# A split-operand product for the first halves of two modulation vectors, and an earlier load of the first projection's weights

## The chip, the cores and the metric

The kernel runs on one core of one Trainium2 chip. The metric is the device time of one execution in microseconds (us). The engines are named as in the profile: PE is TensorE (matrix products and transposes), PEld its weight loads, DVE is VectorE, ACT is ScalarE, POOL is GpSimd, and SP is SyncE, which in this kernel issues the DMAs. L312 is line 312 of the kernel before; the lines behind the change are 9 higher in the kernel after it.

## The reference

One inference step of a hybrid backbone, one layer deep: 128 context tokens and 2048 latent tokens of width 1024, taken here as 17 tiles of 128 tokens (tile 0 is the context). Cut to what matters:

```
def modulation(cond, w_mod, b_mod):                  # cond: 1024 values
    m = silu(cond) @ w_mod + b_mod                   # w_mod: 1024 x 6144
    return split(m, 6)                               # six vectors of 1024

def block(x, s0, mod, ...):
    sh1, sc1, ga1, sh2, sc2, ga2 = mod
    h = rmsnorm(x, norm_mix) * (1 + sc1) + sh1
    o, s_new = mixer(h, s0, ...)                     # one input projection, DeltaNet + gMLP, one output projection
    x = x + ga1 * o
    h = rmsnorm(x, norm_ffn) * (1 + sc2) + sh2
    return x + ga2 * (relu(h @ w_ff1)**2 @ w_ff2), s_new
```

Context and latent tokens have a conditioning vector each, so that each modulation vector comes in two rows. All is in 32-bit floats. Nothing of the mixer can start before h, and so not before `sh1` and `sc1`, the first two of the six vectors.

## The kernel before

**Products.** Large products are made of split operands: a float32 matrix is cast by ACT to the type fp32r (the high part `wH`, L191), DVE subtracts that from the original (the low part `wL`, L192), and PE multiplies high by high, high by low and low by high (`mm3`, L217 to L219), one pass each. `split_w` (L185) makes the two parts of one 128x512 tile. A product of plain float32 operands is a single call, which the trace shows as two passes of PE.

**Modulation vectors.** `scond` holds silu of the two conditioning vectors as eight columns of 128x2. The vectors are made in chunks of 512 columns of `w_mod`, each over eight tiles of 128x512 (256 KB; k0 to k7). The first four chunks are needed first and have their own path. `mod_load` (L306) issues the loads of a chunk: `m0` is the first half of `sh1`, `m1` the first half of `sc1`, `m2` and `m3` the second halves. `mod_columns` (L310) makes eight float32 products with `scond` as the stationary operand into two rows of PSUM (L314), copies them to SBUF on ACT (`mrow`, L316), turns them into columns by four transposes (L319), and adds the bias on DVE (L322; for `sc1` also the weight of the norm, L326). The results are `b1` and `a1`, which scale and shift the normalised tokens.

The chunks 4 to 9 of `w_mod` follow in single steps between the later work. `split_mod_steps` (L329) makes chunk 4, called jc = 4 here: each tile is split, and PE multiplies both parts (L338, L339) with `abW`, a 128x128 stationary operand for each k, most of which is zero. Its columns 32 to 34 hold the high part of `scond` and its columns 64 to 66 the low part (L301 to L304), so that the rows 32 to 34 and 64 to 66 of the result, added, make the two rows wanted. The columns 0 to 32 of `abW` take the small weights `abr` of the mixer, later.

**Tokens.** `xh` (10 rows at the edges of the blocks, L359) and then the tiles of the first block of three (0, 1, 2; loaded at L371) are normalised by `norm_rows` (L291): square and sum on ACT (L297), scale and epsilon on DVE (L175), the power -0.5 on POOL (L176), and the scaling on DVE (L299). The four share three buffers. `first_half` (L384) scales the edge rows by `a1` and `b1`; `column(k)` in `prep_block` (L448) transposes 128 columns of the three token tiles on PE (L461), applies `a1` and `b1` on ACT (L463), and splits the result on DVE (L466, L467). The first projection (`feature_tile`, products L217 to L219 into `pj`) multiplies these by the split tiles of `w_in`, called `W1`, loaded by `load_w1` (L376). The first four of these tiles are `wr` at L713.

**What sets the order.** The kernel names no queue order by hand. The tile framework takes the instructions in program order and orders those of each engine by a time model of its own, within the data's dependences. Buffers of a pool are passed on when their last reader is done: 49 of 128x512 in `wp` (the tiles of m0 to m3 and W1, and the parts of split tiles), four in `sp` ("stage": raw tiles and split parts of jc = 4, and raw tiles of weights that are split on arrival). All loads here go through SP, in one order. The program around the change is the start of the sequence (L707 on):

```
        blk, xs_, cols = prep_block(0)
        ...
        m2 = mod_load(1, 0)
        m3 = mod_load(1, D)
        wr = load_w1(1, range(4))
        mod_columns(m1, 0, a1, vec[:, 8:16], True)
        W1[1] += [split_w(r) for r in wr]
        first_half(0)
```

Ahead of it stand the loads of m0 and m1, `mod_columns` for m0 (L353), and the loads and norms of `xh` and of the three token tiles. Behind it come the other loads of W1, the first four columns of the block with the first products of three feature tiles (L721 to L725), `mod_columns` for m2 and m3 (L726, L727), and the rest of the mixer, block by block.

Of the kernel before, what the change touches and what calls it, by code (L numbers as in the profile page):

```python
# [13 lines left out]
ALU = mybir.AluOpType  # L14
# [5 lines left out]
KT = D // P  # L20
# [41 lines left out]
def hybrid_step(  # L62
# [7 lines left out]
    V, A, G, T = nc.vector, nc.scalar, nc.gpsimd, nc.tensor  # L70
# [12 lines left out]
    def f32(ap):  # L83
        return ap.bitcast(F32)
# [77 lines left out]
    scond = cp.tile([P, KT, 2], F32, name="scond")  # L162
# [6 lines left out]
    def pm1():  # L169
        return pmp.tile([P, 512], F32, tag="pm", name="pm", bufs=2)  # L170
# [9 lines left out]
    def raw_w(src, pool=None, tag="w"):  # L180
        t = (pool or wp).tile([P, 512], F32, tag=tag, name="raw")
        load(out=t, in_=src)
        return t

    def split_w(raw, scale=None, pool=None, tag="w"):  # L185

        h = (pool or wp).tile([P, 512], F32R, tag=tag, name="wH")
        lo = (pool or wp).tile([P, 512], F32R, tag=tag, name="wL")
        if scale is not None:
            V.tensor_scalar_mul(raw, raw, scale)  # L190
        A.copy(h, raw)  # L191
        V.tensor_tensor(out=lo, in0=raw, in1=f32(h), op=ALU.subtract)  # L192
        return h, lo
# [66 lines left out]
    with ExitStack() as ph:  # L260
# [40 lines left out]
        abW = p1.tile([P, KT, P], F32R, tag="abW", name="abW", bufs=1)  # L301
# [4 lines left out]
        def mod_load(half, c0):  # L306
            return [raw_w(w_mod[0, k * P : (k + 1) * P, c0 + half * 512 : c0 + half * 512 + 512])
                    for k in range(KT)]

        def mod_columns(raws, half, dst, bias, scaled):  # L310

            pm = pm1()  # L312
            for k in range(KT):
                T.matmul(pm[0:2, :], scond[:, k, :], raws[k], start=k == 0, stop=k == KT - 1)  # L314
            row = p1.tile([2, 512], F32, tag="mrow", name="mrow", bufs=1)
            A.copy(row, pm[0:2, :])  # L316
            pc = pm1()
            for i in range(4):
                T.transpose(pc[:, 2 * i : 2 * i + 2], row[:, i * P : (i + 1) * P], ident[0:2, 0:2])  # L319
            ks = slice(half * 4, half * 4 + 4)  # L320
            d = dst[:, :, ks]
            V.tensor_tensor(out=d, in0=pc[:, 0:8].rearrange("p (k c) -> p c k", c=2),  # L322
                            in1=bias[:, ks].unsqueeze(1).to_broadcast([P, 2, 4]), op=ALU.add)
            if scaled:
                for cd in range(2):
                    V.scalar_tensor_tensor(out=dst[:, cd, ks], in0=dst[:, cd, ks], scalar=1.0,  # L326
                                           in1=vec[:, 16 + half * 4 : 20 + half * 4], op0=ALU.add, op1=ALU.mult)
# [23 lines left out]
        convw = vec[:, 32:68].rearrange("p (w a) -> p w a", w=3)  # L351
        m1 = mod_load(0, D)
        mod_columns(m0, 0, b1, vec[:, 0:8], False)  # L353


# [20 lines left out]
        def load_w1(gi, ks):  # L376
            return [w1_raw(gi, k) for k in ks]

        def w1_raw(gi, k):
            return raw_w(w_in[0, k * P : (k + 1) * P, gi * 512 : (gi + 1) * 512])  # L380
# [327 lines left out]
        blk, xs_, cols = prep_block(0)  # L708
        for st in xs_:
            st()  # L710
        m2 = mod_load(1, 0)
        m3 = mod_load(1, D)
        wr = load_w1(1, range(4))  # L713
        mod_columns(m1, 0, a1, vec[:, 8:16], True)
        W1[1] += [split_w(r) for r in wr]
        first_half(0)
# [3 lines left out]
        wr = load_w1(0, range(KT))  # L720
        us = [feature_tile(blk, 0, 1, h) for h in range(3)]  # L721
        for k in range(4):
            cols[k]()
            for u in us:
                u["main"][k]()  # L725
        mod_columns(m2, 1, b1, vec[:, 0:8], False)  # L726
        mod_columns(m3, 1, a1, vec[:, 8:16], True)  # L727
        W1[1] += [split_w(r) for r in wk]
# [1015 lines left out]
    raws, sops = {}, {}  # L1744
# [46 lines left out]
    half = [p for p, e in enumerate(seq) if e[1] == NP][0]  # L1791
# [41 lines left out]
    for m, (n, i, u, q) in enumerate(todo):  # L1833
# [12 lines left out]
        h, lo = sops.pop(m)  # L1846
# [72 lines left out]
```

## Time and profile before

| | us |
|---|---|
| three runs | 2704.84, 2711.76, 2714.13 (median 2711.76) |
| profiled execution: its time | 2707.53 |
| profiled execution: its span | 2705.8 |
| products of the MLP (`f`, six groups L217 to L219), busy on PE | 2193.9 |
| products of the input projection (`pj` with `kH`, `kL`, three groups) | 571.4 |
| stretch 0 to 40.4 us of the span: PE busy | 33.41 |

The span is the time from the first to the last recorded instruction of one execution; its mean granted PE clock was 0.99 of full speed. Busy times of an engine's groups may add up to more than the engine's own, because successive products overlap in the records. The profile was read in these views: the page (busy time by engine, the chain of work that ended last), a table of stretches of the span (busy time of each engine, the clock granted to PE, share of the DMA engines and GB/s), and timelines of one engine at a time. In a timeline, a row gives the start and the duration in us (from the first start to the last end of the instructions grouped), the engine, the line, the operation, the result and the operands by their names in the program, shapes, and the count; in brackets stands the idle time of the engine just before, and what ended it. "SPq" is the issue of DMAs on SP.

### The profile page before, as it was taken

Reading aid. Unit: us, or ns where it says so; the run is one execution under the profiler, and the core shown is the slowest. Engines: PE = TensorE matmul, PEld = TensorE weight load, DVE = VectorE, ACT = ScalarE, POOL = GpSimd, SP = SyncE. Lnnn points to the kernel's source line nnn. Section 1 sums busy time; section 2 is a strip of 40 time slices with the busy share of each in tenths; the row PEclk is TensorE's granted clock in tenths of the full one; section 3 lists DMA queues with packets and bytes.
Section 4 is the critical chain, followed back from the end, with each engine's and each line's share of the span. In section 5 each row is a group of like instructions: output and inputs, shape, how many; then the busy total and the mean of one; then the engine's idle time right before and its main releaser. Section 6 shows DMA issues by size and latency. Waiting matters only on the chain.

```text
span 2705.8 us, 45189 instructions
## 1 busy us (share of the span) xinstructions
PE 2632.3 (97%) x15698; PEld 2196.5 (81%) x15698; DVE 1868.0 (69%) x3909; ACT 1246.1 (46%) x3092; POOL 228.2 (8%) x448
## 2 busy tenths in 40 slices
PE   8999998999999999999999999999999999999998
PEld 5999997788887787778888778888888787788887
DVE  5867656877777978985677857565565556775874
ACT  4655555555555667763355533332342432232441
POOL 3111213111111111110000000000000000000000
PEclk9999999999999999999999999999999999999999
DMA  8867539555555657875887786433459979776772
GB/s 296 279 199 223 185 115 294 179 159 155 163 162 172 212 180 245 268 263 175 286 234 232 213 299 206 123 102 109 117 174 371 326 262 308 267 239 216 233 258 91
DMA packets 569387, 580.91 MB, mean 215 GB/s; under 512 B 35692, under 2 KB 401692, under 8 KB 565574
## 3 DMA queue, kind: packets, MB, share of 16 engines
q1 hardware_dynamic: 569158, 578.03, 66.5%
q8 instruction: 123, 2.02, 0.3%
q14 instruction: 106, 0.87, 0.1%
HBM read 398.14 MB, written 179.74 MB: 214 GB/s over the span
## 4 chain that ended last, share of the span: by engine, by line
PE 82%; DMA 7%; DVE 6%; issue 2%; ACT 2%; SPq 1%; POOL 0%; DVEq 0%; POOLq 0%; ACTq 0%
PE f L219 16%; PE f L217 16%; PE f L218 16%; PE pj L217 6%; PE pj L219 6%; PE pj L218 6%; PE pd L952 3%; PE pm L217 1%; DMA qT<-qT_d 1%; PE pm L218 1%; PE pm L219 1%; PE pt L568 1%; PE pd L1129 1%; PE pd L1130 1%; PE pt L528 1%
## 5 line engine op out<-in xcount | busy, mean ns | idle before, releaser
L219 PE MATMUL f<-hop,zL 128*128 128x512 f32 x960 | 377.9, 394 | 1.7 <-DVE zL L1431 1.7
L217 PE MATMUL f<-hop,zH 128*128 128x512 f32 x960 | 377.6, 394 | 1.2 <-ACT zH L1437 1.2
L218 PE MATMUL f<-hop,zH 128*128 128x512 f32 x960 | 378.0, 394 | 0.0
L217 PE MATMUL f<-hop,wH 128*128 128x512 f32 x896 | 356.2, 398 | 5.8 <-ACT wH L1437 5.8
L219 PE MATMUL f<-hop,wL 128*128 128x512 f32 x896 | 352.2, 393 | 0.0
L218 PE MATMUL f<-hop,wH 128*128 128x512 f32 x896 | 352.0, 393 | 0.0
L1437 ACT CAST zH<-zraw 128x512 fp32r<-128x512 f32 x240 | 147.1, 620 | 299.2 <-DVE zraw L1431 91.9
L219 PEld LDWEIGHTS f<-hop,zL 128*128 128x128 f32 x960 | 180.9, 188 | 45.0 <-DVE zL L1431 3.5
L217 PEld LDWEIGHTS f<-hop,zH 128*128 128x128 f32 x960 | 180.7, 188 | 44.7 <-ACT zH L1437 2.9
L218 PEld LDWEIGHTS f<-hop,zH 128*128 128x128 f32 x960 | 180.6, 188 | 40.9
L1431 DVE TENSOR_TENSOR zL<-zraw,zH 128x512 fp32r<-128x512 f32 x240 | 162.6, 687 | 68.2 <-ACT zH L1437 50.8
L217 PEld LDWEIGHTS f<-hop,wH 128*128 128x128 f32 x896 | 169.4, 189 | 40.9 <-ACT wH L1437 6.2
L219 PEld LDWEIGHTS f<-hop,wL 128*128 128x128 f32 x896 | 169.0, 189 | 38.0 <-DVE wL L1431 0.3
L218 PEld LDWEIGHTS f<-hop,wH 128*128 128x128 f32 x896 | 169.4, 189 | 35.2
L217 PE MATMUL pj<-kH,wH 128*128 128x386 f32 (+2 forms) x568 | 191.0, 339 | 0.3 <-DVE kH L466 0.3
L219 PE MATMUL pj<-kH,wL 128*128 128x386 f32 (+2 forms) x568 | 190.6, 336 | 0.0
L218 PE MATMUL pj<-kL,wH 128*128 128x386 f32 (+2 forms) x568 | 189.8, 334 | 0.0
L176 POOL TENSOR_TENSOR r<-rsq,nhalf 128x1 f32<-128x1 f32 (+1 forms) x38 | 23.6, 621 | 1516.4 <-DVE rsq L175 1516.4
L1431 DVE TENSOR_TENSOR wL<-raw,wH 128x512 fp32r<-128x512 f32 x112 | 76.1, 687 | 76.0 <-ACT wH L1437 75.0
L516 DVE SCALAR_TENSOR_TENSOR cv<-pj,vec,cv 128x384 f32<-128x384 f32 (+2 forms) x164 | 87.1, 539 | 59.9 <-ACT cv L513 58.5
L217 PEld LDWEIGHTS pj<-kH,wH 128*128 128x128 f32 x568 | 107.5, 190 | 4.8 <-issue 4.2
L217 PE MATMUL pj<-wH,hH 128*128 128x512 f32 x248 | 110.1, 444 | 0.0
(398 smaller groups left out, 6090.2 us busy)
## 6 DMA issues: line engine op xcount, KB each, us to landing
zraw<-z_d SPq DMA_DIRECT2D x212, 256.0 KB
raw<-in_w_ff_dram SPq DMA_DIRECT2D x128, 256.0 KB
hop<-hop_d SPq DMA_DIRECT2D x28, 1024.0 KB
z_d<-c SPq DMA_DIRECT2D x96, 256.0 KB
zraw<-s_d SPq DMA_DIRECT2D x96, 256.0 KB
raw<-in_w_mod_dram SPq DMA_DIRECT2D x80, 256.0 KB
r<-in_w_ff_dram SPq DMA_DIRECT2D x80, 256.0 KB
s_d<-s SPq DMA_DIRECT2D x64, 256.0 KB
```

The costliest lines, as they stand in the source:

```text
L176: G.tensor_tensor(out=out, in0=t[:np_, :n], in1=nhalf[:np_, :n], op=ALU.pow)
L217: T.matmul(ps, lh, rh, start=first and i == 0, stop=False, skip_group_check=more)
L218: T.matmul(ps, lh, rl, start=False, stop=False, skip_group_check=more)
L219: T.matmul(ps, ll, rh, start=False, stop=last and i == n - 1, skip_group_check=more)
L516: V.scalar_tensor_tensor(out=cv[:, o : o + m], in0=ps[:, s + sh : s + sh + m], scalar=convw[:, w, j : j + 1], in1=cv[:, o : o + m], op0=AL ...
L528: T.transpose(pq[:, i * P : (i + 1) * P], u["x2"][:, i * P : (i + 1) * P], ident)
L568: T.matmul(ps[:, i * P : (i + 1) * P], kTt[:, i * P : (i + 1) * P], rhs[:, i * P : (i + 1) * P], start=True, stop=True)
L952: T.matmul(p[:, h, :], lhs[:, h, :], rhs[:, h, :], start=True, stop=True)
L1129: T.matmul(p[:, h, :], u["qT"][:, h, :], s[:, h, :], start=True, stop=False)
L1130: T.matmul(p[:, h, :], u["QK"][:, h, :], u["vn"][:, h, :], start=s is None, stop=True)
L1431: V.tensor_tensor(out=out, in0=a, in1=b, op=op)
L1437: A.copy(h, src)
```

## The change

In `mod_columns`, the chunks with `half == 0`, which are m0 and m1, are now split tile by tile with `split_w`, and each part is multiplied with `abW` as in `split_mod_steps`, into all 128 rows of PSUM. The two pairs of rows are brought together by a copy on ACT and an addition on DVE. The chunks m2 and m3 are made as before. And in the sequence, the loads of the first four W1 tiles stand ahead of those of m2 and m3.

```
         def mod_columns(raws, half, dst, bias, scaled):

+
             pm = pm1()
-            for k in range(KT):
-                T.matmul(pm[0:2, :], scond[:, k, :], raws[k], start=k == 0, stop=k == KT - 1)
             row = p1.tile([2, 512], F32, tag="mrow", name="mrow", bufs=1)
-            A.copy(row, pm[0:2, :])
+            if half == 0:
+                for k in range(KT):
+                    h, lo = split_w(raws[k])
+                    T.matmul(pm, abW[:, k, :], h, start=k == 0, stop=False)
+                    T.matmul(pm, abW[:, k, :], lo, start=False, stop=k == KT - 1)
+                A.copy(row, pm[32:34, :])
+                V.tensor_tensor(out=row, in0=pm[64:66, :], in1=row, op=ALU.add)
+            else:
+                for k in range(KT):
+                    T.matmul(pm[0:2, :], scond[:, k, :], raws[k], start=k == 0, stop=k == KT - 1)
+                A.copy(row, pm[0:2, :])
             pc = pm1()
             for i in range(4):
                 T.transpose(pc[:, 2 * i : 2 * i + 2], row[:, i * P : (i + 1) * P], ident[0:2, 0:2])
...
         for st in xs_:
             st()
+        wr = load_w1(1, range(4))
         m2 = mod_load(1, 0)
         m3 = mod_load(1, D)
-        wr = load_w1(1, range(4))
         mod_columns(m1, 0, a1, vec[:, 8:16], True)
         W1[1] += [split_w(r) for r in wr]
         first_half(0)
```

The function that it calls is unchanged:

```
    def split_w(raw, scale=None, pool=None, tag="w"):

        h = (pool or wp).tile([P, 512], F32R, tag=tag, name="wH")
        lo = (pool or wp).tile([P, 512], F32R, tag=tag, name="wL")
        if scale is not None:
            V.tensor_scalar_mul(raw, raw, scale)
        A.copy(h, raw)
        V.tensor_tensor(out=lo, in0=raw, in1=f32(h), op=ALU.subtract)
        return h, lo
```

## The prediction

> **What bounds the kernel now.** I read the page's busy times and chain first, then a table of stretches, then the timelines of the first 100 us, engine by engine. The page gives the frame: busy time by engine, and the chain that ended last.
>
> ```profile
> PE 2632.3 (97%) x15698; PEld 2196.5 (81%) x15698; DVE 1868.0 (69%) x3909; ACT 1246.1 (46%) x3092; POOL 228.2 (8%) x448
> ...
> PE 82%; DMA 7%; DVE 6%; issue 2%; ACT 2%; SPq 1%; POOL 0%; DVEq 0%; POOLq 0%; ACTq 0%
> ```
>
> TensorE (PE) is busy for 97% of the span. What a change is worth is therefore the PE time that it saves, less the PE waits that it opens. The stretches around the change (columns: us; busy us of PE, PEld, DVE, ACT, POOL; granted PE clock; DMA share; GB/s):
>
> ```profile
> 0.00:40.40 40.40, 33.41 (x93) 7.82 (x93) 12.20 (x48) 12.59 (x22) 12.75 (x84) 1.00 0.93 325
> 40.40:83.40 43.00, 42.85 (x252) 41.37 (x252) 36.78 (x103) 30.67 (x83) 12.40 (x24) 1.00 0.80 262
> 83.40:86.00 2.60, 0.52 (x3) 0.43 (x3) 0.49 (x1) 1.14 (x3) 0.00 (x0) 1.00 0.42 125
> 86.00:88.00 2.00, 2.00 (x10) 1.75 (x9) 2.00 (x6) 1.94 (x10) 0.00 (x0) 0.60 0.19 55
> 88.00:90.00 2.00, 2.00 (x10) 1.89 (x9) 1.60 (x4) 2.00 (x7) 0.00 (x0) 0.54 0.46 96
> 90.00:200.00 110.00, 110.00 (x672) 105.73 (x671) 80.48 (x158) 63.19 (x192) 20.29 (x71) 1.00 0.76 247
> ```
>
> From 40.4 us on PE has no gap but one, at 83.4 to 85.5, and after that gap it runs for some 3.4 us at a clock of 0.60 and 0.54. So the total is the moment at which the dense part begins, plus the work left then, plus that gap. The head in which the change lies, on PE:
>
> ```profile
> 4.10 8.90 PE L314 MATMUL pm<-raw,scond 128*2 128x512 f32 x16 [4.10 <-DMA raw<-in_w_mod_dram]
> ...
> 14.07 7.03 PE L314 MATMUL pm<-raw,scond 128*2 128x512 f32 x16
> 21.03 0.66 PE L366 MATMUL pt<-ident,xh 10*128 10x10 f32 x8
> ...
> 23.22 7.03 PE L314 MATMUL pm<-raw,scond 128*2 128x512 f32 x16
> 30.97 0.41 PE L319 MATMUL pm<-ident,mrow 2*128 2x2 f32 x4 [0.72 <-ACT mrow L316]
> 31.30 7.03 PE L314 MATMUL pm<-raw,scond 128*2 128x512 f32 x16
> ...
> 39.05 0.41 PE L319 MATMUL pm<-ident,mrow 2*128 2x2 f32 x4 [0.46 <-ACT mrow L316]
> 39.39 0.50 PE L338 MATMUL pm<-wH,abW 128*128 128x512 f32 x1
> 39.73 0.39 PE L339 MATMUL pm<-wL,abW 128*128 128x512 f32 x1
> 40.44 0.59 PE L217 MATMUL pj<-kH,wH 128*128 128x388 f32 x2 [0.32 <-DVE kH L466]
> ```
>
> The four L314 rows are m0, m1, m2 and m3, eight fp32 products each (two passes a product, so x16): 7.03 us where nothing holds them. One follows the other, and the projection (L217) begins at 40.44.
>
> **The change part by part.** Durations are those of the profiled execution.
>
> PE work saved. A product of m0 or m1 costs 7.03 / 8 = 0.88 us; in its place come two one-pass products, each as long as an L338 that has work behind it:
>
> ```profile
> 66.05 0.40 PE L338 MATMUL pm<-wH,abW 128*128 128x512 f32 x1
> 66.28 0.34 PE L217 MATMUL pj<-kH,wH 128*128 128x388 f32 x1
> ```
>
> The next starts 0.23 us later, so 16 x (0.88 - 2 x 0.23) = 6.7 us of PE work go. They are a gain only where PE sets the pace of the head, and after the change it doesn't.
>
> What takes PE's place: the new order of the queues. Program, waits and order are read from the changed kernel as built. ACT gets 16 more casts and DVE 16 more subtractions. ACT casts the tiles k0 to k2 of m1, then squares the third token tile of the first block (call it x2), and only behind that casts k3 to k7. DVE has three subtractions of m1, then x2's mean square, one more subtraction, x2's scaling, and only then the other four. So m1, hence a1, hence all that PE does next (m2 first), hangs on the landing of x2. In the kernel before, m1 needed neither engine, and it ended ahead of x2.
>
> When x2 lands. SP issues in order, and each issue waits until the eighth issue before it has landed.
>
> ```profile
> 11.57 2.96 SPq L359 DMA_DIRECT2D xh<-in_x_sample_dram  x5
> ...
> 15.64 0.35 SPq L371 DMA_DIRECT2D x<-in_x_sample_dram  x1
> 16.47 9.96 SPq L182 DMA_DIRECT2D raw<-in_w_mod_dram  x16
> ...
> 28.20 0.33 SPq L371 DMA_DIRECT2D x<-in_x_sample_dram  x1
> ```
>
> From 11.57 to 16.47 there are seven steps (five xh, two x), each paced by the landing of an m1 tile: 0.70 us for 256 KB. Up to 15.64 SP's order is unchanged. Then come the small projection's weights (a quarter tile), one tile of the next modulation column (jc = 4), wsT, alog, the four W1 tiles that the change moves, three tiles of m2, and x2; the other thirteen tiles of m2 and m3 and the twelve later W1 tiles come behind it. x2 needs alog landed, and xh's buffer, free after the transposes of L366 (which wait for xh's data at some 19 us as before). On DVE (xh scaled, then the second token tile) and ACT:
>
> ```profile
> 18.19 0.74 DVE L299 TENSOR_SCALAR xh<-xh,r 10x1024 f32<-10x1024 f32 x1 [0.66 <-POOL r L176]
> ...
> 21.81 0.75 DVE L299 TENSOR_SCALAR x<-x,r 128x1024 f32<-128x1024 f32 x1 [0.66 <-POOL r L176]
> ```
>
> ```profile
> 13.04 0.57 ACT L316 COPY mrow<-pm 2x512 f32<-2x512 f32 x1 [10.31 <-PE pm L314]
> ...
> 19.81 1.06 ACT L297 ACTIVATE junk<-x 128x1024 bf16<-128x1024 f32 x1 [0.32 <-DMA x<-in_x_sample_dram]
> ...
> 34.16 1.06 ACT L297 ACTIVATE junk<-x 128x1024 bf16<-128x1024 f32 x1 [0.67 <-DMA x<-in_x_sample_dram]
> ...
> 35.21 1.82 ACT L191 CAST wH<-raw 128x512 fp32r<-128x512 f32 x3
> ```
>
> The second token tile is in at 19.8. Behind it 2.25 tiles at 0.70 land by 21.4, alog with them, and x2 is issued at about 21.5. Seven 256 KB tiles are then in flight ahead of it, as many as at the issue of 28.20, which ACT could use at 34.16, 5.96 us later. So x2 is in at 27.5: earlier than before, but m1 now waits for it. One tile more or less in flight moves this by 0.7.
>
> From x2 to m2. The rows for the steps:
>
> ```profile
> 35.34 0.15 DVE L175 TENSOR_SCALAR rsq<-ss 128x1 f32<-128x1 f32 x1 [1.13 <-ACT junk L297]
> ...
> 36.51 0.75 DVE L299 TENSOR_SCALAR x<-x,r 128x1024 f32<-128x1024 f32 x1
> ...
> 56.21 1.88 DVE L192 TENSOR_TENSOR wL<-raw,wH 128x512 fp32r<-128x512 f32 x3
> ```
> ```profile
> 35.58 0.54 POOL L176 TENSOR_TENSOR r<-rsq,nhalf 128x1 f32<-128x1 f32 x1 [7.66 <-DVE rsq L175]
> ```
>
> ACT is free for k3 at 28.55 (34.16 to 35.21 is 1.05), a cast being 0.62. DVE subtracts k3 from 29.2; POOL has the root by 29.5; DVE scales x2 from 29.8, and from 30.45 subtracts k4 to k7 at 0.60 apiece (three take 1.88, the last 0.69), to 32.9. Then in DVE's order three W1 subtractions and two short ones on the small weights stand ahead of the sum of m1's two rows: 3 x 0.60 + 2 x 0.2 = 2.2, so that sum starts at 35.05. PE's last product of m1 (ends 33.3) and ACT's row copy (0.57, to 33.9) fit beside that. The sum of two rows of 512 is in no row of the trace; I bound it by 0.15 (the smallest DVE row above) and 0.69 (the subtraction over as many columns) and take 0.6. With four transposes (0.33 from 30.97 to 31.30) m2 starts at 36.0, against 23.22: **+12.8 us**.
>
> What comes back. Between 23.22 and 40.44 PE had 17.2 us for 2 x 7.03 of products, 2 x 0.33 of transposes and 0.45 of jc = 4: 2.0 us idle. In the new order the first projection products stand between m2 and m3, and row copies and column splits run beside PE's work: **-2.0**. The W1 loads ahead of m2 are worth no more than this: x2 and a1 come later than W1 either way, and m2's and m3's own last tiles (landing by some 31 and 36.5, at 0.70 behind x2) are there before PE asks.
>
> The clock. PE is nearly idle from 12 to 29 us, and for 2.4 us (33.3 to 35.7) ahead of m2. The gap at 83.4 was such a pause, and it cost 2 x (1 - 0.60) + 2 x (1 - 0.54) = 1.7 us of clock behind it. Bounds: 0, as behind the short pauses ahead of 40.44, and 3.4, two such stretches. I take **+1.7**. The Trainium skill (TensorE: Matmul & The Clock Gate, Part 1) lets the clock fall to half only after an idle window of about 3.4 us; the row shows a fall after a pause of 2.08. By that rule m2 would run at full clock, and the sum would be 1.7 lower: a rival below.
>
> The gap at 83.4:
>
> ```profile
> 83.12 0.33 PE L217 MATMUL pj<-kH,wH 128*128 128x388 f32 x1
> 85.53 0.50 PE L338 MATMUL pm<-wH,abW 128*128 128x512 f32 x1 [2.08 <-ACT wH L191]
> ```
> ```profile
> 79.30 0.33 SPq L182 DMA_DIRECT2D raw<-in_w_mod_dram  x1
> ```
> ```profile
> 84.86 0.62 ACT L191 CAST wH<-raw 128x512 fp32r<-128x512 f32 x1 [2.69 <-DMA raw<-in_w_mod_dram]
> ```
>
> It is jc = 4's third tile, issued at 79.30 because four staging buffers are passed round between it and the third projection's weights. In the new order the first two tiles of jc = 4 are loaded and used in the head, so that the chain of buffers is ahead of PE by some 2 to 4 us when the third is due. The gap goes, and the clock loss with it: 2.08 + 1.7 = **-3.8** (0 if another tile of the chain is late in its place).
>
> The sum: 12.8 - 2.0 + 1.7 - 3.8 = **+8.7 us**, 0.32%. Added DVE and ACT time costs nothing more: in 40.4 to 83.4 DVE is busy 36.8 of 43, and the 16 extra splits are over by then. Beyond 200 us the instructions stand in nearly the same order, so I carry nothing on. The profiled execution took 2707.5 (span 2705.8 and 1.7 around it), so it would take 2716.2. The three runs shown have a median of 2711.8, the four executions a mean of 2709.6; I put the sum on the mean: **2718**.
>
> **The rivals.**
> - The gap stays, or another tile of jc = 4 is late: the head's loss and the clock alone, +12.5, 2722. For it: its tiles still pass through four buffers, and each landing took up to 5.5 us (79.30 to 84.86 on ACT). Against it: the first two are early.
> - The clock holds, as by the rule above: +7.0, 2716.6, inside 0.3%.
> - Not slower, by one mechanism: x2 isn't what m1 waits for. DVE gets to x2 at about 25.2 (second token tile scaled by 23.4, some 0.8 later than in its row, as ACT's row copy stands ahead of its square; three subtractions). If x2 were in by then, m1 would end 8 x 0.60 after 23.4, and with the same 3.1 us behind it m2 would start at 31.3: 8.1 - 2.0 - 3.8 = +2.3, 2712, no change that can be told. It decides from a landing 3.5 us after the issue instead of 5.96. Against it: the seven tiles in flight.
> - The change does what it says, and PE sets the head's pace: -6.7, with the gap gone -10.5, 2699. For it: 33.4 us of 40.4 busy before. Against it: DVE's subtractions (0.60) are slower than the new products (0.46 a tile), and DVE has xh and the token tiles in its queue.
>
> **How the numbers follow.** Forecast 0.42; gap stays 0.24; clock holds 0.16; x2 no wait 0.11; PE-paced 0.07. A measurement of this kernel tells 0.3% (8.1 us) from no change. The forecast lies at that bound: 0.26 of it above, 0.16 within. The first rival is all above; the second 0.04 above, 0.12 within; the third 0.09 within, 0.02 faster; the fourth faster. Slower 0.54, same 0.37, faster 0.09. The range leaves out the fourth and some of the tails: from the third less the spread of the executions (about 4 each way), 2708, to the first plus it, 2727.
>
> **What would show it.** Right: ACT's square of the third token tile starting at 27 to 28 after a DMA wait, with m1's casts on both sides of it; PE waiting for wL of m1; m2's products starting at 35 to 37 and their first passes slow (granted clock near 0.5); no PE wait at jc = 4's third tile. Wrong: m2 starting before 32, PE busy from 12 to 29, or a PE wait of over 2 us at jc = 4. It would also be wrong if the difference came from beyond 200 us.

## The result, and the profile after

The changed kernel takes 2722.16 us (median of 8 runs, 2718.79 to 2729.71) against 2711.48 us of the kernel before (8 runs beside them, 2704.84 to 2717.11): 10.7 us more, a ratio of 1.0040 with a 95% interval of 1.0029 to 1.0052. The prediction was 2718, range 2708 to 2727. The profiled execution took 2725.24 us, its span 2723.5.

The page's busy times and its chain of work that ended last, by engine:

```profile
PE 2629.9 (97%) x15698; PEld 2199.0 (81%) x15698; DVE 1876.3 (69%) x3927; ACT 1257.1 (46%) x3108; POOL 226.8 (8%) x448
...
PE 80%; DMA 8%; DVE 7%; ACT 2%; issue 2%; SPq 1%; POOL 1%; DVEq 0%; POOLq 0%; ACTq 0%
```

PE is busy for 2.4 us less than before, while the span is 17.7 us longer in this pair of executions, so PE is idle for 20.1 us more: what was lost is waiting and, within the busy time, slow clock (0.50 below), not work. The stretches of the changed kernel show where (columns as in the prediction):

```profile
0.00:37.07 37.07, 16.61 (x51) 10.92 (x52) 20.17 (x49) 18.82 (x33) 10.23 (x60) 0.79 0.94 332
37.07:42.28 5.21, 5.21 (x8) 0.85 (x8) 4.94 (x18) 4.01 (x8) 3.27 (x9) 0.50 1.06 387
42.28:90.00 47.72, 47.72 (x243) 36.97 (x241) 28.70 (x87) 25.20 (x58) 12.04 (x38) 1.00 0.60 191
90.00:160.00 70.00, 67.19 (x400) 62.72 (x399) 60.11 (x126) 42.86 (x141) 11.94 (x39) 1.00 0.81 254
```

Up to 37.07 PE is busy for less than half of the time (before: 33.41 of 40.40). Then it works without a gap to 90, where the kernel before had its gap at 83.4, but the first 5.21 us run at half clock. Between 90 and 160 it idles for 2.81 us; the kernel before had none there. PE's timeline in the head:

```profile
11.12 0.80 PE L319 MATMUL pm<-wL,abW 128*128 128x512 f32 x1 [5.45 <-DVE wL L192]
...
16.23 0.40 PE L319 MATMUL pm<-wL,abW 128*128 128x512 f32 x1
...
23.37 0.77 PE L318 MATMUL pm<-wH,abW 128*128 128x512 f32 x1
...
29.31 0.79 PE L318 MATMUL pm<-wH,abW 128*128 128x512 f32 x1 [2.97 <-ACT wH L191]
...
34.03 0.63 PE L319 MATMUL pm<-wL,abW 128*128 128x512 f32 x1
36.59 0.55 PE L328 MATMUL pm<-ident,mrow 2*128 2x2 f32 x4 [1.93 <-DVE mrow L321]
37.07 9.60 PE L324 MATMUL pm<-raw,scond 128*2 128x512 f32 x16
```

m0's products, all but the first, run from 11.12 to 16.6, m1's from 23.37 to 34.66 with a pause of 2.97 us in the middle, and m2 (L324) starts at 37.07 instead of 23.22 and takes 9.60 us instead of 7.03. The pause waits for ACT's cast of m1's tile k3. Why that cast is late stands in the timelines of ACT, of SP's issues, and of DVE:

```profile
27.61 1.06 ACT L297 ACTIVATE junk<-x 128x1024 bf16<-128x1024 f32 x1 [4.88 <-DMA x<-in_x_sample_dram]
...
28.66 4.24 ACT L191 CAST wH<-raw 128x512 fp32r<-128x512 f32 x8
```
```profile
21.55 0.40 SPq L380 DMA_DIRECT2D x<-in_x_sample_dram  x1
```
```profile
10.31 0.17 DVE L704 COPY wscale<-vec 128x4 f32<-128x4 f32 x1 [6.54 <-DMA vec<-in_v_columns_dram]
...
29.90 0.75 DVE L299 TENSOR_SCALAR x<-x,r 128x1024 f32<-128x1024 f32 x1
30.57 3.69 DVE L192 TENSOR_TENSOR wL<-raw,wH 128x512 fp32r<-128x512 f32 x6
...
34.70 0.23 DVE L741 CAST abW<-abr 128x128 fp32r<-128x128 f32 x1 [0.44 <-PE pm L319]
...
35.76 0.68 DVE L321 TENSOR_TENSOR mrow<-pm,mrow 2x512 f32<-2x512 f32 x1
```

ACT stands idle for 4.88 us before the square of x2, the third token tile, which was issued at 21.55 and is in at 27.61. The casts of m1's other tiles are queued behind it. On DVE, a small cast that writes into `abW` (L741) waits for m1's last product, and the sum of m1's rows (L321) stands behind that cast. DVE's first row is a wait that the prediction didn't have: a small copy of `vec` stands at the head of its queue and holds m0's subtractions until 10.31.

The waits of PE between 90 and 160 us in the changed kernel (in total, times, longest):

```profile
PE pm L250 <- DVE acc L242: 1.4, 1, 1.4
PE pt L577 <- ACT ev L580: 0.6, 1, 0.6
PE pt L577 <- DVE kTt L568: 0.4, 1, 0.4
PE pt L537 <- ACT junk L548: 0.3, 1, 0.3
```

To compare kernels I use one mark that all of them pass in the same place: the last four products of L250, the end of the modulation chunks 4 to 9. PE's timeline of the kernel before, and of the changed one:

```profile
348.26 1.88 PE L250 MATMUL pm<-acc,pick 128*2 128x512 f32 x4
```
```profile
362.57 1.88 PE L250 MATMUL pm<-acc,pick 128*2 128x512 f32 x4
```

At the mark the changed kernel is 14.3 us behind; the other 3.4 us of the pair's 17.7 come later.

### The profile page after: what moved, and what is told of

Same layout as the page of the kernel before. It is cut to its first block, busy times and chain, and to the rows that moved or that the text cites. A ratio compares the mean times of both kernels' runs of the same rounds, so it can differ in the third digit from the quotient of the medians.

```text
span 2723.5 us, 45259 instructions
## 1 busy us (share of the span) xinstructions
PE 2629.9 (97%) x15698; PEld 2199.0 (81%) x15698; DVE 1876.3 (69%) x3927; ACT 1257.1 (46%) x3108; POOL 226.8 (8%) x448
## 4 chain that ended last, share of the span: by engine, by line
PE 80%; DMA 8%; DVE 7%; ACT 2%; issue 2%; SPq 1%; POOL 1%; DVEq 0%; POOLq 0%; ACTq 0%
PE f L219 16%; PE f L217 16%; PE f L218 16%; PE pj L217 6%; PE pj L219 6%; PE pj L218 5%; PE pd L961 2%; PE pm L217 1%; PE pm L218 1%; PE pm L219 1%; DMA qT<-qT_d 1%; DMA raw<-in_w_mod_dram 1%; PE pd L1138 1%; PE pd L1139 1%; PE pt L577 1%
```

## The experiments

**Theory**: the loss is m1's splits, queued on ACT and DVE among the norms of the token tiles, so that m1 hangs on x2's landing; PE's halved clock adds to it. **Rivals**: the moved W1 loads; the pace of the subtractions; m0's late row. The runs were timed in three sets (e1 to e4, e5 to e8, e9 to e12), each beside the kernel before. "Mark" is the start of the four L250 products; "more" is the median less that of before beside it. The ratio is not that of the two medians, so the two columns can differ by some 2 us (e4: 0.37% is 10.0 us, where the medians differ by 7.7).

| run | m2 starts | mark | more, us | ratio (95%) |
|---|---|---|---|---|
| before, first profile | 23.22 | 348.26 | | |
| changed kernel | 37.07 | 362.57 | +10.7 | 1.0040 (1.0029 to 1.0052) |
| e1 loads moved, no split | 23.56 | 352.19 | +4.3 | 1.0014 (1.0005 to 1.0023) |
| e2 split, loads not moved | 37.33 | 359.69 | +15.6 | 1.0059 (1.0045 to 1.0072) |
| e3 changed, x2 loaded early | 32.79 | 356.67 | +7.7 | 1.0034 (1.0022 to 1.0047) |
| e4 changed, only m0 split | 30.86 | 355.41 | +7.7 | 1.0037 (1.0025 to 1.0050) |
| e5 changed, x2's norm behind m1 | 32.16 | 359.57 | +10.3 | 1.0044 (1.0031 to 1.0057) |
| e6 changed, `vec` wait gone | 36.38 | 360.06 | +10.3 | 1.0039 (1.0026 to 1.0052) |
| e7 m2 and m3 split instead | 37.32 | 356.96 | +13.3 | 1.0049 (1.0037 to 1.0062) |
| e8 both early loads, no split | 24.55 | 356.17 | +15.7 | 1.0056 (1.0042 to 1.0070) |
| e9 changed, PE kept busy | 38.49 | 365.37 | +21.3 | 1.0077 (1.0064 to 1.0090) |
| e10 changed, only m1 split | 35.03 | 364.75 | +16.9 | 1.0065 (1.0050 to 1.0081) |
| e11 before, five staging buffers | 23.13 | 351.11 | -0.2 | 1.0000 (0.9990 to 1.0009) |
| e12 before, second profile | 23.99 | 350.66 | +0.1 | 0.9998 (0.9988 to 1.0007) |

**e1, the loads alone.**

```
         # the kernel before
+        wr = load_w1(1, range(4))
         m2 = mod_load(1, 0)
         m3 = mod_load(1, D)
-        wr = load_w1(1, range(4))
```

> The kernel before with only the loads of the first four W1 tiles moved ahead of those of m2 and m3; nothing is split. Theory (the loss is m1's splits queued behind the third token tile x2): the loads of m2 and m3 land some 2.8 us later but PE still finds them there, so m2 starts at 23.2 as before, the wait at jc = 4's third tile stays, and the time is that of before within 3 us (2709 to 2714). Rival (the earlier W1 loads delay what PE needs): m3's last tiles or x2 come late, the dense part begins 3 us or more after 40.4, and the time is over 2715.

+4.3 us, the mark 3.9 us (against the second profile of before 1.5 us) later. m2 starts as before, so the theory holds for that; the time, 2714.26, is just over what it allowed. The row of m2, PE's timeline of e1:

```profile
23.56 8.72 PE L314 MATMUL pm<-raw,scond 128*2 128x512 f32 x16
```

m2 took 8.72 us instead of 7.03: one stretch at half clock, which the second profile of before (e12) has too. The move by itself gains nothing.

**e2, the split alone.** The changed kernel with the line `wr = load_w1(1, range(4))` put back behind `m3`.

> The changed kernel with the W1 loads put back behind m2 and m3; only the split of m0 and m1 is left. Theory: x2 still goes out with seven 256 KB tiles in flight ahead of it and m1's casts still stand on both sides of its square, so x2's square starts at 27 to 28 and m2 at 35.5 to 37; 2719 to 2723, that is, all of the loss is in this half of the change. Rival (the loss comes from the moved loads): m2 starts before 33 and the time is below 2716.

2725.6 us, +15.6, x2's square at 28.49, m2 at 37.33: all of the loss is in the split. Each number is a little over its expected range, the time by 2.6 us. In the head e2 is 2.9 us better than the changed kernel, in the time it isn't; the two intervals overlap.

**e3, x2 loaded early.**

```
-        xh = p1.tile([P, D], F32, tag="x", name="xh", bufs=3)[0:10, :]
+        xh = p1.tile([P, D], F32, tag="xh", name="xh", bufs=1)[0:10, :]
```

> The changed kernel, but xh has a buffer of its own, so that x2 need not wait for xh's buffer: it is loaded right behind the second token tile, and its square and scaling stand ahead of m1's splits instead of among them. Theory (m1 waits for x2's landing): x2 is squared at 20 to 21, m1's subtractions end at about 29 instead of 33, m2 starts at 31 to 32.5 instead of 37.1, and the time falls by 5 to 7.5 us to 2714.5 to 2717. It stays above before, as m1's splits still run behind the token tiles. Rival (the subtractions' own pace is the loss, and x2 only stands in the gaps): m2 starts after 35 and the time is 2720 to 2723.

ACT's and PE's timelines of e3:

```profile
21.78 1.06 ACT L297 ACTIVATE junk<-x 128x1024 bf16<-128x1024 f32 x1 [0.99 <-DMA x<-in_x_sample_dram]
```
```profile
32.48 0.38 PE L328 MATMUL pm<-ident,mrow 2*128 2x2 f32 x4 [1.93 <-DVE mrow L321]
```

x2 is squared 5.8 us earlier, m2 starts 4.3 us earlier, the mark comes 5.9 us earlier. The time is 3.0 us shorter by the medians (7.7 instead of 10.7 over before), 1.6 by the ratios; each was timed in a set of its own, and the intervals overlap, so a gain in the time is not shown. Each number is a little over its expected range, and in the head the direction is the theory's: m1 waited for x2. What stays at 32.79 is m1's split behind three norms, and its sum behind splits of W1 (the 1.93 us).

**e4, only m0 split.** `if half == 0 and not scaled:`

> The changed kernel with only m0 split; m1 is a plain float32 product again. Theory: m1 no longer needs ACT or DVE. m0's row is still late (its last product ends at 16.6 instead of 13.0), so m1 starts at about 20.8, runs 7.0 us and some 1.7 more at a halved clock, and m2 starts at 29.5 to 31: 6 to 7 us sooner than in the changed kernel, 2713.5 to 2716.5. Rival (what costs is m0's late row and the idle clock, not m1's splits): m2 starts after 34 and the time stays at 2719 or more.

PE's timeline of e4:

```profile
19.59 0.66 PE L375 MATMUL pt<-ident,xh 10*128 10x10 f32 x8 [3.34 <-DVE rsq L175]
20.85 0.48 PE L328 MATMUL pm<-ident,mrow 2*128 2x2 f32 x4 [0.60 <-DVE mrow L321]
21.27 8.59 PE L324 MATMUL pm<-raw,scond 128*2 128x512 f32 x16
```

m2 starts at 30.86, inside the expected range, 6.2 us sooner than with both. The time, 2717.7, is 1.2 us over it. m0's split alone already costs 7.6 us at m2: m1, which ran from 14.07 before, now stands behind xh's transposes and m0's row in PE's queue.

**e10, only m1 split.** `if half == 0 and scaled:`

> The changed kernel with only m1 split; m0 is a plain float32 product again and ends at 13 as before. In the built order the casts of k0 to k6 stand ahead of x2's square and only k7's behind it, and x2 goes out behind four W1 tiles and seven of m2. Theory (one tile of m1 behind x2 is enough): x2 is squared at 29 to 30.5, m2 starts at 34 to 36, and the time is 2717.5 to 2721.5, nearly the loss of both splits. Rival (the losses of the two halves add up, m0's 7.7 as measured with m0 alone and some 3 of m1): m2 starts before 29 and the time is 2712 to 2715.

ACT's and PE's timelines of e10:

```profile
29.50 1.06 ACT L297 ACTIVATE junk<-x 128x1024 bf16<-128x1024 f32 x1 [4.42 <-DMA x<-in_x_sample_dram]
```
```profile
35.03 9.99 PE L324 MATMUL pm<-raw,scond 128*2 128x512 f32 x16
...
88.56 0.44 PE L217 MATMUL pj<-kH,wH 128*128 128x388 f32 x1 [1.84 <-DVE cv L525]
```

As expected, one tile behind x2 is enough (squared at 29.5, m2 at 35.0). But the time was missed: 2728.95 instead of at most 2721.5. m2 takes 9.99 us, more than half of it at half clock, and a wait of 1.84 us with another half-clock stretch behind it stays at 88.6, where the changed kernel has none. The losses of the halves (7.7 and 16.9) don't add up to that of both (10.7).

**e5, x2's norm pinned behind m1.** The load isn't moved; x2's square is issued behind m1's row copy on ACT, its mean and scaling behind m1's sum on DVE (`row_copy` and `row_sum` stand for these two instructions).

```
-        for x in xs0:
+        for x in xs0[:2]:
             norm_rows(x)
...
         mod_columns(m1, 0, a1, vec[:, 8:16], True)
+        with tc.issue_after(row_copy), tc.issue_after(row_sum):
+            norm_rows(xs0[2])
```

> The changed kernel with the loads in their changed order, but the norm of x2 (the third token tile) pinned behind m1's row copy on ACT and behind the sum of m1's rows on DVE; x2's load is not moved. Theory (m1 waits only because x2's square and scaling stand ahead of its splits in the two queues): m1's eight subtractions run from 21.3 to 28.5 without a break, PE's last product of m1 ends at 29 to 30, m2 starts at 31 to 32.5, and the halved clock is over by then as PE is busy through a whole window; the time falls by 4 to 6 us to 2716 to 2718. Rival (x2 is late for the first columns as well, so that what m1 gains is lost again at the first transposes): m2 starts at 32 but the time stays at 2720 or more.

m2 starts at 32.16, as the theory had it, 4.9 us sooner. But 3.0 us of it are left at the mark and none in the median time: the outcome that I had put with the rival, though not for its reason, since PE doesn't wait at the first columns. The waits of PE from 33 to 160 us in e5:

```profile
PE pm L250 <- DVE acc L242: 2.0, 1, 2.0
PE pt L579 <- ACT ev L582: 1.2, 1, 1.2
PE pm L330 <- ACT mrow L327: 0.4, 1, 0.4
PE pt L579 <- ACT junk L550: 0.4, 1, 0.4
```

Lines stand 2 higher in e5: the waits at L250 and for `ev` are those of the changed kernel, and longer (2.0 and 1.2 us instead of 1.4 and 0.6). Behind the longest, at L250, the clock fell as well. The stretches of e5 around it:

```profile
133.82:137.23 3.41, 1.39 (x10) 1.12 (x9) 3.39 (x7) 0.63 (x2) 0.00 (x0) 1.00 1.05 354
137.23:140.64 3.41, 3.41 (x7) 1.74 (x8) 3.41 (x7) 1.05 (x2) 0.00 (x0) 0.50 0.85 266
```

That settles where the 4.9 us shrink to 3.0: between 90 and 160 us e5 idles for 1.1 us more than the changed kernel (3.89 against 2.81), waits 0.4 us at L330 and loses 1.7 us of clock behind L250, and it gains 1.3 us because m2 takes 8.34 us instead of 9.60. The wait at L250 is for DVE, and from 125 to 140 us DVE is busy for 14.98 of 15 us: it sets the pace there, and PE, arriving earlier, waits. Where the 3.0 us go behind the mark isn't settled.

**e6, the wait for `vec`.** `tc.keep_in_program_order(...)` around the copy of `wscale` from `vec`.

> The changed kernel, but the small copy of wscale from vec, which stands at the head of DVE's queue and holds m0's subtractions until vec has landed at 10.3, is kept behind them. The prediction's chain has nothing of this wait. Theory (m1 waits for the token tiles and x2, not for m0): m0's products end at 11 to 12 instead of 16.6, but m2 starts at 36 to 37.5 as before, and the time is that of the changed kernel within 3 us (2719 to 2725). Rival (m0's late row is part of the loss): m2 starts before 34 and the time is below 2718.

PE's timeline of e6:

```profile
11.09 0.49 PE L319 MATMUL pm<-wL,abW 128*128 128x512 f32 x1
```

m0's last product ends at 11.6 instead of 16.6; m2 starts at 36.38, the time is 2721.87. The wait that the prediction left out is hidden behind x2's.

**e9, PE kept busy while it waits.**

```
                     T.matmul(pm, abW[:, k, :], lo, start=False, stop=k == KT - 1)
+                    if scaled and k == 2:
+                        for _ in range(9):
+                            T.matmul(pm, zW, lo, start=False, stop=False)   # zW is zero
```

> The changed kernel with nine more products in m1, behind those of its third tile, whose stationary operand is all zero: they add zero and only keep PE busy while it waits for x2. Theory (a part of the loss is PE's halved clock): PE is busy from 23.3 to 29 or 30, a whole stretch of 3.4 us, so that the clock is full again at 30 at the latest; m1's last product ends at 33 to 34 instead of 34.7, m2 starts at 35.7 to 36.7 and runs 7.0 us instead of about 9.6 in all, and the time falls by 2.5 to 4 us to 2717.5 to 2720. Rival (the clock is the same for the time, since m2 would else wait for its tiles): m2 takes as long, or the next step waits instead, and the time stays at 2721 or more.

PE's timeline of e9:

```profile
27.87 2.98 PE L325 MATMUL pm<-wL,zW 128*128 128x512 f32 x9
...
38.19 0.38 PE L334 MATMUL pm<-ident,mrow 2*128 2x2 f32 x4 [3.05 <-DVE mrow L327]
38.49 8.72 PE L330 MATMUL pm<-raw,scond 128*2 128x512 f32 x16
```

A miss: +21.3. The clock did come back, at 29.5. But the loads landed 0.9 to 1.7 us later in this execution (the square of xh at 17.28 instead of 16.39, that of the first token tile at 19.51 instead of 17.86), the sum of the rows still stood behind DVE's splits, and in that pause of 3.05 us the clock fell again. m2 takes 8.72 us. So the run doesn't price the clock. Of the 10.6 us that it takes more than the changed kernel 2.8 are there at the mark; the rest is later and stays unexplained.

**e7 and e8, versions meant to beat the kernel before.** e7: the changed kernel with `if half == 1:` and xh's own buffer. e8: e7's two early loads in the kernel before, no split.

> The kernel before, with three edits: m2 and m3 are split instead of m0 and m1, the first four W1 tiles are loaded ahead of them, and xh has a buffer of its own, so that x2 is loaded early. Theory (a split is worth something only where PE and not the landing of the tiles sets the pace, and where the two other engines have no late work ahead of it): m0 and m1 end as in the kernel before, the first products of the projection run at 25 to 33 while m2 and m3 land, m3's last product ends at 37 to 39, and the time is 4 to 7 us below before, 2703 to 2706. Rival (16 more subtractions on DVE cost as much as the products save, wherever they stand): no faster than before, 2709 to 2714.

> The kernel before with the two moves of loads alone (W1 ahead of m2 and m3; xh in a buffer of its own, so that x2 is loaded early) and no split. Theory: the first products stand among m2's while its tiles land, which takes back the 2.0 us that PE idled ahead of 40.4 and little more, as m2 and m3 still cost 14 us of PE: 2707 to 2711. Rival (the early loads alone make the gain of the run with m2 and m3 split): 2706 or less.

Both were slower, by 13.3 and 15.7 us. In e7 the head goes as planned up to the first products (PE 26.7 to 37), but m3's split ends at 46.9 instead of 37 to 39, and then PE waits once for 5.30 us. PE's and ACT's timelines of e7:

```profile
72.83 0.66 PE L217 MATMUL pj<-kH,wH 128*128 128x388 f32 x1 [5.30 <-DVE cv L525]
```
```profile
67.99 1.06 ACT L423 ACTIVATE junk<-x 128x1024 bf16<-128x1024 f32 x1 [4.20 <-DMA x<-in_x_sample_dram]
```

It is the same mechanism in the next block: the square of a token tile (L423) that hasn't landed stands in ACT's queue, here ahead of the convolution (`cv`) for which PE waits. e8 has no split and passes 100 us about level with the kernel before, waits 2.82 us on `cv` at 133.56, is 7.9 us late at the mark, and loses the rest later. Where those 8 us go isn't settled.

**e11, the gap at jc = 4 alone.** `NS = 5`, and `bufs=48` for the large pool.

> The kernel before with five staging buffers instead of four (and 48 instead of 49 of the large pool, for room). Theory (the wait of 2.08 us at jc = 4's third tile comes from four buffers passed round): that tile is loaded earlier, the wait and the half clock behind it go, and the time is 2.5 to 4.5 us below before, 2706.5 to 2709. Rival (the wait is the landing's, or the next tile of the chain is late in its place): a wait of over 1 us on a tile of jc = 4 or of the third projection's weights stays, and the time is that of before within 2 us.

PE's waits from 60 to 160 us in e11:

```profile
PE pm L250 <- DVE acc L242: 2.0, 1, 2.0
PE pm L338 <- ACT wH L191: 1.3, 1, 1.3
```

The wait at 85.5 is gone: the cause of the gap was the four buffers. But the time is that of before (1.0000). The sixth tile of jc = 4 is late instead (1.33 us at 93.0), and L250's products wait 2.04 at 128.7. The rival was right about the sum.

**e12, before once more.**

> The kernel before, unchanged, for a second profile of it. The profiled execution of the prediction took 2707.5, 4 us less than the median of its runs. Theory (those 4 us lie in the late stages, whose short waits and half-clock stretches differ from one execution to the next): up to 400 us the second profile agrees with the first within 1 us, and it is longer by 1 to 6 us between 400 and 1100 us. Rival (they lie in the head, and the change's loss there is smaller than the two first profiles show): m2 or the dense part starts 2 us or more later than in the first profile.

This execution took 2716.0 us, 8.5 more than the first. Both theory and rival have a part: 2.4 us lie ahead of the mark (m2 took 8.72 us at half clock, dense part at 42.90 instead of 40.44), 6.1 behind it. So a pair of profiles is good for places, and no better than some 8 us for the total; the 10.7 is from the medians.

**What the runs show together.** The split alone makes all of the loss (e2, +15.6); the moved loads alone cost 4.3 us (e1), and beside the split no cost of theirs shows. In the head, m1 waits for x2, and m2 starts sooner when x2 is out of the way (e3, e5). How much of the 10.7 us is x2's wait is not shown: e3 and e5 start m2 4.3 and 4.9 us sooner, and neither is faster than the changed kernel clear of the noise. Splitting m0 alone costs 7.7 us without that wait (e4).

## Why the prediction was right

The sign was right, and so was the mechanism in the head. The size came out close, +8.7 forecast, +10.7 measured (7.9 to 14.1 by the interval), and in part by luck (last step). By its steps:

- **x2 decides.** In at 27.5 forecast, squared at 27.61; casts of m1 on both sides of it. e3 shows it by moving x2.
- **m2 at +12.8**: +13.85. The 1.1 us are mostly in m1's end. I let DVE's subtractions set it (33.3); they ended at 33.0, but PE's products stood 0.43 us apart at half clock and ended at 34.66, and the sum of the rows waited for them (L741). The price of the clock belonged in m1 too.
- **Idle time that comes back, -2.0.** PE has no gap from 37.07 to 90. The pauses of before there were 0.72 + 0.46 + 0.32 = 1.5; my 2.0 took jc = 4's products at 0.45 us (39.39 to 40.12 is 0.73) and left out a transpose at 38.26.
- **The clock, +1.7**: +2.6, half of 5.21 us. The rival by which the clock holds was wrong. But "PE is nearly idle from 12 to 29 us" was wrong as well: it was busy for 9.11 of these 17 us, as m0's late products and m1's first three tiles ran there, so this term came out better than its reason. The rule in the Trainium skill (TensorE: Matmul & The Clock Gate, Part 1) names an idle window; here the clock fell after windows in which PE worked for 40% (below).
- **The gap at jc = 4, -3.8.** It went, as forecast (no gap between 42.28 and 90). But "0 if another tile of the chain is late in its place" was nearer: 2.81 us of new waits at 109 to 142, none of them on jc = 4. This is the term that I had too good, and e11 shows the same exchange.
- **Sum up to the mark**: 13.85 - 1.5 + 2.6 - 3.8 + 2.8 = 14.0, against 14.3 (first profile of before) or 11.9 (second).
- **Nothing beyond 200 us.** Not shown either way: from the mark to the end the changed kernel takes 2360.9, before 2357.5 and 2363.6. The prediction called the gap at 83.4 the only one from 40.4 us on; that holds for its stretches, which end at 200 us. Behind them PE idles for another 64 us in the kernel before, so that what the head loses need not arrive at the end.
- **The total.** The head lost 14.3 us at the mark (11.9 by the second profile), where I had 8.7 in all. From the mark to the end the profiles of all the runs range from 2354.3 us (e6) to 2370.2 (e8), and a shift of the head doesn't carry through: e2 passes the mark 2.9 us before the changed kernel and comes out at +15.6, e5 passes it 3.0 us before and comes out at +10.3. That the medians differ by 10.7, 2 us from the forecast, is closer than its terms were.

Two things the prediction said in passing fit too: the 6.7 us of PE work that go were no gain in this head, and the moved W1 loads gain nothing by themselves (e1, +4.3). Beside the split they may: +10.7 with them, +15.6 without (e2), with intervals that overlap.

## What to carry to other kernels

A queue is only as early as its latest landing: before moving work to another engine, read in its built order what stands ahead, and when that lands. Work saved on the busiest engine counts only in stretches that it paces; this head is paced by landings. And time won early can be given back at the next stretch that another engine paces (e5; e11 gave its gain back at other waits), so a local gain of some us is to be checked at a mark well behind it, and on medians.

## What the runs showed of the hardware

The granted clock changes in steps of 3.41 us. The stretches between its steps (columns as above), first in the changed kernel, then in e3 and e6:

```profile
18.39:21.80 3.41, 1.39 (x13) 1.02 (x13) 2.93 (x8) 3.39 (x8) 0.95 (x2) 1.00 0.95 303
...
28.63:32.04 3.41, 2.73 (x6) 1.61 (x7) 2.90 (x6) 3.41 (x9) 0.55 (x1) 0.50 1.05 386
32.04:35.45 3.41, 2.62 (x7) 1.53 (x5) 2.97 (x7) 1.61 (x4) 0.00 (x0) 0.50 1.06 387
...
38.87:42.28 3.41, 3.41 (x6) 0.51 (x4) 3.32 (x9) 2.72 (x6) 3.27 (x9) 0.50 1.05 386
42.28:45.70 3.42, 3.42 (x10) 0.65 (x8) 1.39 (x2) 0.62 (x1) 3.42 (x18) 1.00 0.98 346
```
```profile
24.98:28.40 3.42, 3.42 (x9) 2.63 (x10) 3.42 (x7) 3.42 (x8) 0.00 (x0) 0.50 1.06 392
28.40:31.81 3.41, 2.15 (x10) 1.40 (x8) 3.03 (x8) 1.46 (x4) 0.00 (x0) 1.00 1.06 388
31.81:35.22 3.41, 2.74 (x10) 0.83 (x11) 3.31 (x13) 1.31 (x3) 0.00 (x0) 1.00 1.05 386
```
```profile
22.31:25.73 3.42, 2.94 (x7) 1.90 (x7) 2.23 (x4) 0.60 (x2) 0.00 (x0) 0.50 1.06 406
25.73:29.14 3.41, 0.15 (x1) 0.00 (x0) 0.15 (x1) 1.67 (x4) 0.26 (x1) 1.00 1.04 392
```

The clock halved behind windows with 1.39 us of PE work (changed kernel, after 21.80; e5, after 137.23). It held behind one with 2.15 (e3, after 31.81). No threshold comes out between them: windows with 1.65 us (changed kernel, 14.97 to 18.39) and 1.66 (e10, 27.38 to 30.79) held the clock, and one with 1.75 (e12, 20.88 to 24.29) lost it. Once low, it stayed low behind windows with 2.73 and 2.62, and rose behind windows that were busy throughout (42.28; e3, 28.40) or for 2.94 (e6, 25.73). The window's length is that of the Trainium skill's page (TensorE: Matmul & The Clock Gate, Part 1); an idle window isn't needed to lose the clock, and 80% of one doesn't win it back. For a kernel with short pauses this is the costlier half: in the changed kernel six windows in a row ran at half clock.
